# Fourteen pairs of distances between split weights and operands in a dense encoder kernel

## The chip, the cores and the metric

The kernel runs on one core of one Trainium2 chip. The metric is the device time in microseconds of one execution, from the first to the last instruction plus what the launch adds around it; lower is better. A profile of one execution stands beside the times. Engines are named as the profile names them: PE is TensorE (PEld its weight loads), DVE is VectorE, ACT is ScalarE, POOL is GpSimd, SP is SyncE.

## The reference

Two layers over a sequence of 256 positions and 2048 channels, all in float32. Each layer does:

```python
hn = _rmsnorm(h, norm_g[i])
u = hn @ w_in[i]                      # 2048 -> 5632 columns
a_val, a_glu, a_z, q, k, v, b_z = jnp.split(u, offs, axis=-1)
ya = _conformer_conv(a_val, a_glu, conv_w[i], conv_b[i], cln_g[i], cln_b[i])
ya = ya * jax.nn.silu(a_z)
yb = _window_attention(q, k, v, bias_band, sink[i]) * jax.nn.silu(b_z)
h = h + jnp.concatenate([ya, yb], axis=-1) @ w_out[i]
e = _rmsnorm(p[i] @ w_pe[i], pe_g[i])
h = h + e * jax.nn.sigmoid(h @ w_pg[i])
```

`_conformer_conv` is a gated linear unit, a depthwise convolution of width 31, a layer norm and a SiLU; `_window_attention` is banded attention with 16 query heads over 4 key heads. A final RMSNorm closes the trunk. Nearly all of the work is in the four projections `w_in`, `w_out`, `w_pe` and `w_pg`.

## The kernel before

**Layout.** Everything is transposed: channels lie on the 128 partitions, the 256 positions along the free axis. A projection is a sum over 128-channel slices; the weight slice (128x128) is the stationary operand, which TensorE loads, and the activations (128x256) are the moving operand, which it streams.

**Three matmuls for one.** A float32 product is made of three faster fp32r matmuls. Each operand is split into a rounded high part and the low part that is left. `mm3` (L396) issues high x high, high x low and low x high, in that order, into one PSUM accumulation; "high x low" is the high part of the weights with the low part of the activations. So of three weight loads two are of the high part of the weights and one of the low part.

**Half tiles.** The weights come as a list of 156 half tiles for each layer (`HALVES`, made by `weight_halves`), 1024 float32 per partition each, mostly 8 slices of 128 columns. One half tile is 24 matmuls: 8 slices by 3. In the order of the list: 0 to 3 `w_pe`; 4 to 35 value and gate columns of the convolution group (tile ag); 36 to 39 keys (k); 40 to 43 values (v); 44 to 75 attention gate and queries (zb, q); 76 to 91 convolution gate (za); 92 to 107 `w_out` with the attention half (o<-yb); 108 to 123 `w_out` with the convolution half (o<-ya); 124 to 155 `w_pg` (g). In layer 0, half tiles 0 to 3 are used unsplit.

**The weights' way.** `load` (L158) fetches two half tiles in one transfer of 1 MB on the SP queue into one of three raw buffers. `split` (L163) takes one of five buffers of the tile w, has ACT cast the raw values to the high part (L168) and DVE subtract to the low part (L171). `ahead` and `get` (L178 to L195) run the splits up to four half tiles before their use. The order of DVE, PE and ACT instructions is written out by hand; `pump` (L203) is called after each half tile and issues convolution taps (L559) and pieces of the attention between the splits. `step` and `steps` (L406 to L422) walk the cursor over the half tiles and call `mm3`.

**Where things lie.** A buffer of w is 2 x 1024 + 64 float32 (8,448 bytes) per partition and begins at a multiple of 128 bytes. The split starts `SHIFT` = 16 elements, 64 bytes, into it: high part at 64, low part 4,096 bytes further. The activations' split tiles (hg, ya, yb, h1, and pp for `w_pe` in layer 1) begin at multiples of 128 bytes, and each slice of them is 1,024 bytes long. So the address phase modulo 128 of every slice of the activations is 0 and that of every slice of the weights, high or low, is 64. For the values (v) the roles are exchanged: the activations are loaded and the weights streamed. Small tiles lie elsewhere: qq (split queries, loaded) and keys (streamed) at 32, s (loaded for the transposes pt) at 96, ident and ones at 64.

```python
        w = wspl.tile([P, 2 * HALF + 64], F32R, tag="w", name=f"w{h}")
        w = w[:, SHIFT:SHIFT + 2 * HALF].rearrange("p (t n) -> p t n", t=2)
        hi, lo = w[:, 0], w[:, 1]
        nc.scalar.copy(hi, raw)
```

Of the kernel before, what the change touches and what calls it, by code (L numbers as in the profile page):

```python
# [10 lines left out]
F32 = mybir.dt.float32  # L11
# [6 lines left out]
P = 128  # L18
# [10 lines left out]
W_KV = NKV * HD  # L29
# [9 lines left out]
HALF = 1024  # L39
# [9 lines left out]

NB_FIRST = KT  # L50
NSPL = 5
SHIFT = 16
MAN = 'DVE,PE,Activation'
LY = (2, 1)
ORD = 1
# [65 lines left out]
NHALF = len(HALVES)  # L121
# [8 lines left out]
def trunk_kernel(ctx: ExitStack, tc: tile.TileContext, xT, pT, wst, par, gain, relb, sinkp, onehot, out):  # L130
    nc = tc.nc
# [11 lines left out]
    def bigt(name, dt=F32):  # L143

        return big.tile([P, 2, 8, S], dt, tag="big", name=name)

    def halves(t):
        return [t[:, 0], t[:, 1]]

    def bank(name):  # L150
        return ps.tile([P, 2, S], F32, tag="ps", name=name)
# [3 lines left out]
    raws, spl = {}, {}  # L155
# [7 lines left out]
    def split(h):  # L163
        raw = raws[h // 2][:, h % 2, :]
        w = wspl.tile([P, 2 * HALF + 64], F32R, tag="w", name=f"w{h}")
        w = w[:, SHIFT:SHIFT + 2 * HALF].rearrange("p (t n) -> p t n", t=2)
        hi, lo = w[:, 0], w[:, 1]
        nc.scalar.copy(hi, raw)  # L168
        spl[h] = w
        if h not in (4, 5):  # L170
            nc.vector.tensor_sub(lo, raw, hi.bitcast(F32))  # L171

    def first_lo(h):

        w = spl[h]
        nc.vector.tensor_sub(w[:, 1], raws[h // 2][:, h % 2, :], w[:, 0].bitcast(F32))

    def ahead(h):  # L178

        while state["spl"] < min(h, TOT - 1):  # L180
            n = state["spl"] + 1
            while state["raw"] < min(n // 2 + LD - 1, TOT // 2 - 1):
                state["raw"] += 1
                load(state["raw"])
            if HALVES[n % NHALF][0] != "w_pe" or n >= NHALF:
                split(n)
            state["spl"] = n

    def get(h):

        r = h % NHALF
        if r < 12:
            ahead(h + (r | 1) + 2 - r)
        else:
            ahead(h + LS)  # L195
        return spl.pop(h)
# [6 lines left out]
    def pump(taps=None):  # L203
        taps = RATES[(Cursor.h % NHALF > 4 + 32 + 8 + 12) + (Cursor.h % NHALF > 4 + 32 + 8 + 32 + 4)] if taps is None else taps
        state["credit"] += taps
        if ORD:
            sides()
        while state["credit"] >= 1 and conv_q:
            g = conv_q.pop(0)
            try:  # L210
                next(g)
                state["credit"] -= 1
                conv_q.insert(1, g)
            except StopIteration:
                pass
        if not conv_q:
            state["credit"] = 0.0
        if not ORD:
            sides()
# [59 lines left out]
    h = halves(bigt("x"))  # L279
# [95 lines left out]
    def fold(a):  # L375
        t = wk.tile([P, S], F32, name="fold", tag="sg")
        nc.vector.tensor_add(t, a[:, 0, :], a[:, 1, :])
        return t

    def halves_of(a):  # L380
        return [a[:, 0, :], a[:, 1, :]]

    def square_acc(acc, src, first, eng=None):

        if first:
            nc.scalar.activation(acc, src, AF.Square)
            return
        sq = wk.tile([P, 2, S], F32, name="sq", tag="sq", bufs=3)
        nc.scalar.activation(sq, src, AF.Square)
        (eng or nc.gpsimd).tensor_add(acc, acc, sq)  # L390
# [5 lines left out]
    def mm3(o, w, x, start, stop):  # L396


        nc.tensor.matmul(o, w[:, 0], x[:, 0], start=start, stop=False, skip_group_check=True)  # L399
        nc.tensor.matmul(o, w[:, 0], x[:, 1], start=False, stop=False, skip_group_check=True)  # L400
        nc.tensor.matmul(o, w[:, 1], x[:, 0], start=False, stop=stop, skip_group_check=True)  # L401

    class Cursor:
        h = 0

    def step(o, X, start, stop):  # L406

        steps([o], X, [start], stop)

    def steps(os, X, starts, stop):  # L410

        parts = []
        for _ in os:
            name, _, k0, nk = HALVES[Cursor.h % NHALF]
            parts.append(get(Cursor.h).rearrange("p t (k c) -> p t k c", k=nk))
            Cursor.h += 1
        for kk in range(nk):
            k = k0 + kk
            for o, w, start in zip(os, parts, starts):
                mm3(o, w[:, :, kk, :], X[k // 8][:, :, k % 8, :], start and kk == 0, stop and kk == nk - 1)  # L420
        for _ in os:
            pump()  # L422

# [13 lines left out]
    for l in range(DEPTH):  # L437
# [4 lines left out]
        hg = []  # L442
# [16 lines left out]
        def operands(k, n):  # L459
            for k in range(k, k + 2 * n, 2):  # L460
                subs.append(operand(k))
                if len(subs) > 1:
                    subs.pop(0)()

        ecopy = []
        for q in range(4):
            n = Cursor.h
            Cursor.h += 1
            if l:
                w = get(n).rearrange("p t (j k c) -> p t j k c", j=4, k=2)  # L470
            else:
                raw = raws[n // 2][:, n % 2, :].rearrange("p (j k c) -> p j k c", j=4, k=2)
            for jj in range(0, 4, 2):
                j = 4 * q + jj
                b = bank("e")
                for x in range(2):
                    for k in range(2):
                        if l:
                            mm3(b[:, x, :], w[:, :, jj + x, k, :], pp[:, :, k, :], x == 0 and k == 0, k == 1)
                        else:  # L480
                            nc.tensor.matmul(b[:, x, :], raw[:, jj + x, k, :], pf[:, k, :], start=x == 0 and k == 0,
                                             stop=k == 1, skip_group_check=True)
                if l == 0 and j // 2 < 4:
                    for k in (4 * (j // 2), 4 * (j // 2) + 2):
                        if k < KT - 2:
                            square_acc(hacc, h[k // 8][:, k % 8:k % 8 + 2, :], k == 0, nc.vector)
                    if j // 2 == 3:
                        sq = wk.tile([P, 2, S], F32, name="sq", tag="sq", bufs=3)
                        nc.scalar.activation(sq, h[1][:, 6:8, :], AF.Square)
                        hparts = [fold(hacc)] + halves_of(sq)  # L490
                if j // 2 == QQ[l][0]:
                    dg = rstd_col(hparts, D, f"rh{l}")
                    ahead(4 if l == 0 else Cursor.h - 1 - q + 5)
                if j // 2 == QQ[l][1]:
                    rbs.append(rstd_row(dg, f"rh{l}", copy=False))
                    if l == 0:
                        first_lo(4)
                        ahead(5)
                        operands(0, 1)
                        first_lo(5)  # L500
                        subs.pop(0)()
                        operands(2, 1)
                if QQ[l][1] + (l == 0) <= j // 2 <= QQ[l][1] + 1:
                    operands(4 * (j // 2 - QQ[l][1]), 2)
                ecopy.append((j, b))

                while ecopy and (l or j // 2 >= 3):
                    jc, bc = ecopy.pop(0)
                    nc.scalar.copy(e[jc // 8][:, jc % 8:jc % 8 + 2, :], bc)
            pump()  # L510
# [34 lines left out]
        a, zb = halves(az)  # L545
# [42 lines left out]
        b = pair(hg, f"k{l}")  # L588
# [8 lines left out]
        vb = [bank(f"v{l}_{b}") for b in range(2)]  # L597
        for q in range(4):
            n = Cursor.h
            Cursor.h += 1  # L600
            w = get(n).rearrange("p t (k c) -> p t k c", k=4)
            for kk in range(4):
                k = 4 * q + kk
                for b in range(2):
                    mm3(vb[b][:, 0, :], hg[k // 8][:, :, k % 8, b * P:(b + 1) * P], w[:, :, kk, :],
                        k == 0, k == KT - 1)
            pump()
        v = wk.tile([P, 2, W_KV], F32, name=f"v{l}", tag="v", bufs=1)
# [60 lines left out]
        for i in range(0, 8, 2):  # L669

            b = pair(hg, f"zb{l}_{i}")
            nc.scalar.activation(zb[:, i:i + 2, :], b, AF.Silu)
            b = pair(hg, f"q{l}_{i}")
# [3 lines left out]
            for hh in range(2):  # L677
                r, o = rows_of[hh], rows_of[1 - hh]
# [7 lines left out]
        for t in range(0, NCT, 2):  # L686
            b = pair(hg, f"za{l}_{t}")
# [59 lines left out]
        for j in range(0, KT, 2):  # L747
            b = bank(f"o{l}_{j}")
# [6 lines left out]
        for j in range(0, KT, 2):  # L755
# [3 lines left out]
            hi, lo = (x[:, j % 8:j % 8 + 2, :] for x in halves(h1[-1]))  # L759
            b = bank(f"o{l}_{j}")  # L760
# [50 lines left out]
        for j in range(0, KT - 2, 2):  # L811
            if j:
                b = pair(h1, f"g{l}_{j}")
            else:
                b = bank(f"g{l}_{j}")
# [4 lines left out]
            if j == 4 and not last:  # L820
                pp = wk.tile([P, 4 * S + 32], F32R, name="pp", tag="qq")
                pp = pp[:, 24:24 + 4 * S].rearrange("p (x k s) -> p x k s", x=2, k=2)
                hilo(pp[:, 0], pp[:, 1], pf)
        for j in range(KT - 2, KT):
            b = bank(f"g{l}_{j}")[:, 0:1, :]
# [4 lines left out]
        h = e  # L830
# [93 lines left out]
```

## Time and profile before

| | us |
|---|---|
| runs of the kernel | 951.45, 951.17, 944.24 |
| median | 951.17 |
| the profiled execution | 950.28 |
| its span, first to last instruction | 948.5 |
| mean granted TensorE clock in it | 0.997 of full speed |

The page puts the span into busy shares of the engines, a strip of 40 time slices, the DMA queues, the chain of work that ended last, and groups of instructions by line and tile. A group such as `g<-h,w` names the tile written and the tiles read. Bytes moved are 182.55 MB, 192 GB/s over the span. The strip shows TensorE at nine tenths or more in all slices but the first and the last:

```profile
PE   8999999999999999999999999999999999999995
PEld 7999999999999999999999999999999999999995
DVE  3899999998887676776679998999888878677663
ACT  4655455787875554454466444558787555546551
```

Since matmuls are pipelined, "busy" says only that at least one was under way. How many matmuls a stretch holds says how fast TensorE went through it.

### The profile page before, as it was taken

What the parts mean: (1) busy time and instruction counts of PE and PEld (TensorE: products, weight loads), DVE (VectorE), ACT (ScalarE), POOL (GpSimd) and SP (SyncE); (2) the same over time, 40 slices, a digit from 0 to 9 for tenths busy, and PEclk for the clock granted to TensorE, in tenths of its full rate; (3) what the DMA queues carried; (4) which work ended last, traced back from release to release, by engine and by line L of the source; (5) the groups of instructions that cost most, each with busy time, mean ns of one, the idle gap of its engine ahead of it and who ended that gap; (6) DMA issues with size and microseconds to landing.
All of it is one profiled execution on the core that took longest, in us unless ns stands there. A gap on an engine that the chain in (4) does not pass through costs nothing.

```text
span 948.5 us, 19102 instructions
## 1 busy us (share of the span) xinstructions
PE 935.5 (99%) x7952; PEld 918.8 (97%) x7952; DVE 769.4 (81%) x1290; ACT 549.4 (58%) x830; POOL 83.8 (9%) x79
## 2 busy tenths in 40 slices
PE   8999999999999999999999999999999999999995
PEld 7999999999999999999999999999999999999995
DVE  3899999998887676776679998999888878677663
ACT  4655455787875554454466444558787555546551
POOL 0022001010000000011103200000100010000111
PEclk9999999999999999999999999999999999999998
DMA  8674556555456465556555566465454564655532
GB/s 294 226 254 157 200 178 244 195 188 191 168 174 231 171 224 183 178 179 225 189 196 198 174 219 206 154 217 199 167 205 144 190 223 146 246 186 178 191 121 90
DMA packets 29011, 182.55 MB, mean 192 GB/s; under 512 B 3595, under 2 KB 4156, under 8 KB 9084
## 3 DMA queue, kind: packets, MB, share of 16 engines
q1 hardware_dynamic: 24284, 165.70, 49.9%
q0 software_dynamic: 3344, 12.88, 4.2%
q10 hardware_dynamic: 1296, 2.75, 0.8%
q8 instruction: 62, 1.02, 0.4%
q14 instruction: 25, 0.20, 0.1%
HBM read 177.09 MB, written 4.23 MB: 191 GB/s over the span
## 4 chain that ended last, share of the span: by engine, by line
PE 95%; DVE 3%; DMA 1%; issue 0%; ACT 0%; POOL 0%; ACTq 0%; DVEq 0%
PE g L401 6%; PE g L399 6%; PE g L400 6%; PE ag L401 6%; PE ag L399 6%; PE ag L400 6%; PE o L400 6%; PE o L399 6%; PE o L401 6%; PE za L399 3%; PE zb L400 3%; PE za L400 3%; PE zb L401 3%; PE zb L399 3%; PE q L399 3%; PE za L401 3%
## 5 line engine op out<-in xcount | busy, mean ns | idle before, releaser
L171 DVE TENSOR_TENSOR w<-raw,w 128x1024 fp32r<-128x1024 f32 x306 | 373.2, 1228 | 105.1 <-ACT w L168 104.5
L168 ACT CAST w<-raw 128x1024 fp32r<-128x1024 f32 x308 | 316.2, 1046 | 166.3 <-PE ag L401 40.6
L559 DVE SCALAR_TENSOR_TENSOR cz<-az,pars,cz 128x241 f32<-128x241 f32 (+11 forms) x480 | 217.8, 502 | 1.0
L401 PE MATMUL ag<-hg,w 128*128 128x256 f32 x512 | 143.0, 279 | 0.6 <-DVE w L171 0.5
L399 PE MATMUL ag<-hg,w 128*128 128x256 f32 x512 | 142.8, 279 | 0.0
L401 PE MATMUL g<-h,w 128*128 128x256 f32 x512 | 142.6, 279 | 0.0
L399 PE MATMUL g<-h,w 128*128 128x256 f32 x512 | 142.6, 278 | 0.0
L400 PE MATMUL g<-h,w 128*128 128x256 f32 x512 | 142.6, 278 | 0.0
L400 PE MATMUL ag<-hg,w 128*128 128x256 f32 x512 | 142.5, 278 | 0.0
L401 PEld LDWEIGHTS ag<-hg,w 128*128 128x128 f32 x512 | 96.2, 188 | 1.2 <-DVE w L171 1.0
L401 PEld LDWEIGHTS g<-h,w 128*128 128x128 f32 x512 | 97.2, 190 | 0.0
L400 PEld LDWEIGHTS ag<-hg,w 128*128 128x128 f32 x512 | 96.9, 189 | 0.1
L399 PEld LDWEIGHTS ag<-hg,w 128*128 128x128 f32 x512 | 96.1, 188 | 0.9 <-ACT w L168 0.8
L399 PEld LDWEIGHTS g<-h,w 128*128 128x128 f32 x512 | 96.1, 188 | 0.0
L400 PEld LDWEIGHTS g<-h,w 128*128 128x128 f32 x512 | 96.1, 188 | 0.0
L399 PE MATMUL o<-yb,w 128*128 128x256 f32 x256 | 72.2, 282 | 0.0
L399 PE MATMUL za<-hg,w 128*128 128x256 f32 x256 | 72.0, 281 | 0.0
L400 PE MATMUL o<-yb,w 128*128 128x256 f32 x256 | 71.6, 280 | 0.0
L399 PE MATMUL q<-hg,w 128*128 128x256 f32 x256 | 71.5, 279 | 0.0
L401 PE MATMUL o<-yb,w 128*128 128x256 f32 x256 | 71.4, 279 | 0.0
L399 PE MATMUL zb<-hg,w 128*128 128x256 f32 x256 | 71.4, 279 | 0.0
L399 PE MATMUL o<-ya,w 128*128 128x256 f32 x256 | 71.3, 278 | 0.0
(219 smaller groups left out, 2269.4 us busy)
## 6 DMA issues: line engine op xcount, KB each, us to landing
raw<-in_wst SPq DMA_DIRECT2D x153, 1024.0 KB, 4.9
bias<-fscr POOLq DMA_DIRECT2D x16, 384.0 KB, 4.0
raw<-in_wst SPq DMA_DIRECT2D x4, 512.0 KB, 8.0
az<-in_xT POOLq DMA_DIRECT2D x4, 512.0 KB, 5.3
hscr<-e POOLq DMA_DIRECT2D x2, 1024.0 KB, 5.5
az<-hscr POOLq DMA_DIRECT2D x4, 512.0 KB, 5.8
x<-in_xT SPq DMA_DIRECT2D x3, 512.0 KB, 8.2
out_t<-og ACTq DMA_DIRECT2D x4, 256.0 KB, 3.0
```

The source lines that it names most:

```text
L168: nc.scalar.copy(hi, raw)
L171: nc.vector.tensor_sub(lo, raw, hi.bitcast(F32))
L399: nc.tensor.matmul(o, w[:, 0], x[:, 0], start=start, stop=False, skip_group_check=True)
L400: nc.tensor.matmul(o, w[:, 0], x[:, 1], start=False, stop=False, skip_group_check=True)
L401: nc.tensor.matmul(o, w[:, 1], x[:, 0], start=False, stop=stop, skip_group_check=True)
L559: nc.vector.scalar_tensor_tensor(acc[:, t, lo_:hi_], a[:, t, lo_ + s:hi_ + s], w(k), acc[:, t, lo_:hi_], ALU.mult, ALU.add)
```

## The change

The two parts of a split half tile get places of their own. `SHIFT` becomes a pair of byte distances, one for the high and one for the low part, and `shift(h)` picks the pair for half tile h: in each layer seven groups of sixteen consecutive half tiles have a pair from `SHIFTS`, all others have (64, 64). The low part is counted from element `HALF + 32`, so at equal distances it lies 4,224 bytes behind the high one. The size of the buffer is the same. The rest of the diff hands the two parts on as a pair of tiles where one tile with two halves was handed on before; the matmuls and their order are the same.

```diff
-SHIFT = 16
+SHIFT = (64, 64)
+SHIFTS = [
+    [(4, 16, 16), (20, 48, 48), (76, 80, 80), (92, 96, 96), (108, 112, 112), (124, 64, 0), (140, 0, 64)],
+    [(4, 64, 96), (20, 96, 64), (76, 64, 32), (92, 32, 64), (108, 64, 80), (124, 80, 64), (140, 48, 64)],
+]
+
+
+def shift(h):
+
+    for k, a, b in SHIFTS[h // NHALF]:
+        if k <= h % NHALF < k + 16:
+            return a // 4, b // 4
+    return SHIFT[0] // 4, SHIFT[1] // 4
...
     def split(h):
         raw = raws[h // 2][:, h % 2, :]
         w = wspl.tile([P, 2 * HALF + 64], F32R, tag="w", name=f"w{h}")
-        w = w[:, SHIFT:SHIFT + 2 * HALF].rearrange("p (t n) -> p t n", t=2)
-        hi, lo = w[:, 0], w[:, 1]
+        a, b = shift(h)
+        hi, lo = w[:, a:a + HALF], w[:, HALF + 32 + b:2 * HALF + 32 + b]
         nc.scalar.copy(hi, raw)
-        spl[h] = w
+        spl[h] = (hi, lo)
...
     def mm3(o, w, x, start, stop):
 
 
-        nc.tensor.matmul(o, w[:, 0], x[:, 0], start=start, stop=False, skip_group_check=True)
-        nc.tensor.matmul(o, w[:, 0], x[:, 1], start=False, stop=False, skip_group_check=True)
-        nc.tensor.matmul(o, w[:, 1], x[:, 0], start=False, stop=stop, skip_group_check=True)
+        nc.tensor.matmul(o, w[0], x[0], start=start, stop=False, skip_group_check=True)
+        nc.tensor.matmul(o, w[0], x[1], start=False, stop=False, skip_group_check=True)
+        nc.tensor.matmul(o, w[1], x[0], start=False, stop=stop, skip_group_check=True)
```

More of the change, by code (lines that the diff above doesn't have):

```diff
@@ L173, in first_lo @@
     def first_lo(h):
-        w = spl[h]
-        nc.vector.tensor_sub(w[:, 1], raws[h // 2][:, h % 2, :], w[:, 0].bitcast(F32))
+        hi, lo = spl[h]
+        nc.vector.tensor_sub(lo, raws[h // 2][:, h % 2, :], hi.bitcast(F32))
     def ahead(h):
@@ L396, in mm3, with parts_of @@
     def mm3(o, w, x, start, stop):
-        nc.tensor.matmul(o, w[:, 0], x[:, 0], start=start, stop=False, skip_group_check=True)
-        nc.tensor.matmul(o, w[:, 0], x[:, 1], start=False, stop=False, skip_group_check=True)
-        nc.tensor.matmul(o, w[:, 1], x[:, 0], start=False, stop=stop, skip_group_check=True)
+        nc.tensor.matmul(o, w[0], x[0], start=start, stop=False, skip_group_check=True)
+        nc.tensor.matmul(o, w[0], x[1], start=False, stop=False, skip_group_check=True)
+        nc.tensor.matmul(o, w[1], x[0], start=False, stop=stop, skip_group_check=True)
+    def parts_of(x):
+        return [x[:, 0], x[:, 1]]
     class Cursor:
@@ L414, in steps @@
             name, _, k0, nk = HALVES[Cursor.h % NHALF]
-            parts.append(get(Cursor.h).rearrange("p t (k c) -> p t k c", k=nk))
+            parts.append(get(Cursor.h))
             Cursor.h += 1
@@ L419, in steps @@
             for o, w, start in zip(os, parts, starts):
-                mm3(o, w[:, :, kk, :], X[k // 8][:, :, k % 8, :], start and kk == 0, stop and kk == nk - 1)
+                mm3(o, [y[:, kk * P:(kk + 1) * P] for y in w], parts_of(X[k // 8][:, :, k % 8, :]),
+                    start and kk == 0, stop and kk == nk - 1)
         for _ in os:
@@ L469, in trunk_kernel @@
             if l:
-                w = get(n).rearrange("p t (j k c) -> p t j k c", j=4, k=2)
+                w = [y.rearrange("p (j k c) -> p j k c", j=4, k=2) for y in get(n)]
             else:
@@ L478, in trunk_kernel @@
                         if l:
-                            mm3(b[:, x, :], w[:, :, jj + x, k, :], pp[:, :, k, :], x == 0 and k == 0, k == 1)
+                            mm3(b[:, x, :], [y[:, jj + x, k, :] for y in w], parts_of(pp[:, :, k, :]), x == 0 and k == 0, k == 1)
                         else:
@@ L600, in trunk_kernel @@
             Cursor.h += 1
-            w = get(n).rearrange("p t (k c) -> p t k c", k=4)
+            w = get(n)
             for kk in range(4):
@@ L604, in trunk_kernel @@
                 for b in range(2):
-                    mm3(vb[b][:, 0, :], hg[k // 8][:, :, k % 8, b * P:(b + 1) * P], w[:, :, kk, :],
+                    mm3(vb[b][:, 0, :], parts_of(hg[k // 8][:, :, k % 8, b * P:(b + 1) * P]),
+                        [y[:, kk * W_KV:(kk + 1) * W_KV] for y in w],
                         k == 0, k == KT - 1)
```

## The prediction, made before the changed kernel was run

> **What bounds the kernel now.** I read the page first: busy times, the chain that ended last, the costliest groups.
>
> ```profile
> span 948.5 us, 19102 instructions
> ...
> PE 935.5 (99%) x7952; PEld 918.8 (97%) x7952; DVE 769.4 (81%) x1290; ACT 549.4 (58%) x830; POOL 83.8 (9%) x79
> ...
> PE 95%; DVE 3%; DMA 1%; issue 0%; ACT 0%; POOL 0%; ACTq 0%; DVEq 0%
> ...
> L171 DVE TENSOR_TENSOR w<-raw,w 128x1024 fp32r<-128x1024 f32 x306 | 373.2, 1228 | 105.1 <-ACT w L168 104.5
> L168 ACT CAST w<-raw 128x1024 fp32r<-128x1024 f32 x308 | 316.2, 1046 | 166.3 <-PE ag L401 40.6
> ...
> L401 PE MATMUL ag<-hg,w 128*128 128x256 f32 x512 | 143.0, 279 | 0.6 <-DVE w L171 0.5
> ```
>
> TensorE carries 95% of the chain and the waits in front of it are parts of a microsecond. The 279 ns of a matmul is its latency; matmuls overlap, so what counts is the step from one start to the next, which I call the pace. The timeline of a quiet stretch shows it.
>
> ```profile
> 100.00 0.28 PE L400 MATMUL ag<-hg,w 128*128 128x256 f32 x1
> 100.01 0.19 PEld L401 LDWEIGHTS ag<-hg,w 128*128 128x128 f32 x1
> 100.11 1.23 DVE L559 SCALAR_TENSOR_TENSOR cz<-az,pars,cz 128x241 f32<-128x241 f32 x3
> 100.12 0.28 PE L401 MATMUL ag<-hg,w 128*128 128x256 f32 x1
> 100.12 0.19 PEld L399 LDWEIGHTS ag<-hg,w 128*128 128x128 f32 x1
> 100.23 0.28 PE L399 MATMUL ag<-hg,w 128*128 128x256 f32 x1
> ```
>
> Each weight load (PEld) starts 0.01 us or less behind a matmul and belongs to the next one: the load reads w while the matmul reads the operand. So the change can act in one place, the pace, if these two reads disturb each other. To see whether the pace varies, I cut the span at the first matmuls of the fourteen groups that the change moves (window view; 16 half tiles of 24 matmuls = 384 matmuls in each, in the order of the change's two lists; the windows' counts take in a few neighbours).
>
> ```profile
> 23.79:70.65 46.86, 46.23 (x388) 44.68 (x387) 43.43 (x68) 28.28 (x37) 5.89 (x5) 1.00 0.70 240
> 70.65:114.17 43.52, 43.52 (x386) 43.52 (x385) 43.45 (x70) 21.69 (x27) 9.06 (x6) 1.00 0.52 175
> 239.43:293.86 54.43, 54.43 (x464) 51.68 (x463) 44.37 (x93) 38.44 (x72) 2.56 (x4) 1.00 0.54 186
> 293.86:340.66 46.80, 46.71 (x396) 46.48 (x395) 35.71 (x45) 26.27 (x37) 2.68 (x3) 1.00 0.51 182
> 340.66:385.89 45.23, 45.23 (x386) 45.23 (x385) 29.85 (x33) 20.45 (x23) 0.00 (x0) 1.00 0.58 208
> 385.89:431.12 45.23, 45.23 (x387) 45.23 (x385) 34.48 (x45) 22.16 (x25) 2.59 (x2) 1.00 0.53 182
> 431.12:476.34 45.22, 45.22 (x386) 45.22 (x385) 29.69 (x33) 21.45 (x26) 5.79 (x5) 1.00 0.60 215
> 488.54:533.58 45.04, 45.04 (x387) 44.92 (x386) 41.58 (x58) 27.95 (x38) 11.00 (x6) 1.00 0.48 164
> 533.58:578.88 45.30, 45.30 (x393) 45.30 (x392) 45.23 (x81) 19.70 (x24) 4.75 (x3) 1.00 0.61 209
> 704.11:758.70 54.59, 54.59 (x464) 51.84 (x463) 44.45 (x94) 38.45 (x72) 0.56 (x1) 1.00 0.48 166
> 758.70:804.46 45.76, 45.67 (x397) 45.44 (x396) 34.65 (x45) 26.16 (x37) 2.69 (x3) 1.00 0.53 179
> 804.46:847.98 43.52, 43.52 (x387) 43.52 (x386) 30.75 (x34) 20.48 (x23) 0.00 (x0) 1.00 0.62 225
> 847.98:891.50 43.52, 43.52 (x387) 43.52 (x386) 32.74 (x45) 24.08 (x30) 2.59 (x2) 1.00 0.54 187
> 891.50:935.02 43.52, 43.52 (x387) 43.52 (x385) 24.24 (x30) 21.17 (x31) 5.17 (x4) 1.00 0.30 105
> ```
>
> Columns: window and length, busy time and count of PE, PEld, DVE, ACT, POOL, granted clock, DMA share, GB/s. The clock is 1.00 throughout and TensorE is never idle in the pure stretches, yet the same code has two paces. The w_out and w_pg stages of layer 0 (340.66 to 476.34) take 45.23 us for 384 matmuls, 117.8 ns each; the same stages of layer 1 (804.46 to 935.02) take 43.52 us, 113.3 ns, with the same addresses. DVE and DMA do not explain it: in 70.65:114.17 DVE is busy for 43.45 of 43.52 us and the pace is the fast one. So at a distance of 64 bytes TensorE runs in one of two locked paces, 4.5 ns apart. I take the four windows at 43.52 us as 113.3 ns, the four from 293.86 to 476.34 as 117.8 (the first holds a gap besides) and the six others, which hold attention matmuls or gaps and, by their times, both paces, as the middle, 115.5. The mean over the fourteen is (4 x 113.3 + 4 x 117.8 + 6 x 115.5) / 14 = 115.5 ns.
>
> **Is there a price of the address distance?** All groups stand at 64 bytes, so the answer must come from neighbours. In the layout, qq (loaded) and keys (streamed) both start 32 bytes past a multiple of 128: distance 0. The transposes load s at 96 and stream ident at 64: distance 32. The idle matmuls load ones and stream ident, both at 64: distance 0. First two lines of the chain in layer 0 and one in layer 1:
>
> ```profile
> 176.28 0.95 PE sc L627 x8
> ...
> 179.95 0.87 PE pt L654 x8
> ...
> 629.07 0.95 PE sc L627 x8
> ```
>
> And a window over the idle matmuls near the end:
>
> ```profile
> 935.57:936.47 0.90, 0.90 (x10) 0.90 (x9) 0.74 (x2) 0.09 (x1) 0.00 (x0) 1.00 0.00 0
> ```
>
> The scores, at distance 0, take 0.95 / 8 = 119 ns for the same 128x256 shape: 1 above the slow pace and 6 above the fast one. Eight in a row is little, since a lock may need longer. Of the 128-wide ones, transposes at 32 take 0.87 / 8 = 109 ns; the idle matmuls at 0 take 0.90 us for eight steps, 112 ns (its count of 10 includes one at each end). Both pairs say that distance 0 is dearer, by 3 to 6 ns, and the second that 32 is not. The two score rows use the two qq buffers, which lie 4,224 bytes apart, an odd multiple of 128: equal times, so 128 more changes nothing here, and I take the phase modulo 128.
>
> **The change, part by part.**
> - Number of instructions, DMAs, waits, their order: unchanged. The same casts, subtractions and matmuls, on other offsets in the same w tile. No queue is passed by anything.
> - Writes of the split at other offsets (L168, L171): all offsets are multiples of 16 bytes. Nearest rows are the taps of the convolution, whose starts differ by multiples of 4 bytes:
>
> ```profile
> L559 DVE SCALAR_TENSOR_TENSOR cz<-az,pars,cz 128x255 f32<-128x255 f32 x32 | 15.2, 475 | 0.0
> L559 DVE SCALAR_TENSOR_TENSOR cz<-az,pars,cz 128x253 f32<-128x253 f32 x32 | 15.2, 474 | 0.0
> L559 DVE SCALAR_TENSOR_TENSOR cz<-az,pars,cz 128x254 f32<-128x254 f32 x32 | 15.1, 472 | 0.0
> ```
>
> They agree within 3 ns of 475, so I put the split at no change: at most 1% of 1228 ns, about 12 ns per half tile either way, covered by TensorE's 2.7 us per half tile. Where DVE is full (70.65:114.17), that cover is thin: 224 subtractions x 12 ns = 2.7 us would be the most if every one showed. I take 0.
> - The low part's default start moves from 4,096 to 4,224 bytes behind the high one: nothing, by the score rows. Bound: the difference of the two paces, 4.5 ns, on a third of the matmuls outside the groups (7,392 - 5,376 = 2,016): 672 x 4.5 ns = 3 us either way.
> - The distances: 14 x 384 = 5,376 matmuls, so 1 ns of mean pace is 5.4 us. Bounds for each group: 113.3 (fast lock) and 119.4 (distance 0). In mm3 two of three loads read the high part, so it weighs 2/3 and the low part 1/3. For each distance I take the nearest row: 64, 48, 80: both locks occur, 115.5. 32: also 115.5, since the transposes show no price there. 16 and 112, only 16 bytes from 0: 119.4. 96, as far from 0 as from 64 and with no row: the middle, 117.5. 0: 119.4.
>
> Layer 0: (16,16) 119.4; (48,48) 115.5; (80,80) 115.5; (96,96) 117.5; (112,112) 119.4; (64,0) 2/3 x 115.5 + 1/3 x 119.4 = 116.8; (0,64) 118.1. Layer 1: (64,96) 116.2; (96,64) 116.8; (64,32), (32,64), (64,80), (80,64), (48,64) 115.5 each. Sum 1,632.7, mean 116.6, that is 1.1 ns above 115.5, 6 us. Against the profiled execution, 950.28 us (span 948.5 and 1.8 around it, 0.9 below the median 951.17): 950.28 + 6 = 956 us. A slower TensorE gives every other engine more slack; where it became faster than 113.3, DVE would be late next in 70.65:114.17.
>
> **Rivals.**
> 1. The distance does nothing; the paces are a matter of how the two streams happen to lock after a disturbance. For it: both paces at one and the same distance, and three runs of one program from 944.24 to 951.45. Against it: the score and idle rows. Mean pace stays 115.5: 950 us, with the spread of the runs. The Trainium skill says so too (TensorE: Matmul & The Clock Gate, Step-by-step: what each phase is for): matmul operand and weight load have read ports of their own, and loading the next weights takes no bandwidth from the running matmul. By that the change is worth nothing. The trace disagrees in part: 112 against 109 ns in like matmuls. The same page's spacing for isolated matmuls (Back-to-back issue gap: N / 2.4 + 2.5 ns, 109.2 at 256 columns) would make 384 matmuls 41.9 us, an estimate; no window here reaches it.
> 2. Faster: the fourteen switches of distance shake TensorE out of the slow lock, and it stays in the fast one in all groups: 2.2 x 5.376 = 12 us less, 938 us. It decides, by the bound below, once 8.6 of these 12 us come. Against it: the slow lock held for 135 us in layer 0, and the change also touches the stretch that is fast now.
> 3. Clearly slower: every distance other than 64 meets more collisions than 64, and each mixed pair takes the price of its worse half: 119.4 or more everywhere. 3.9 x 5.376 = 21 us, 971 us; above that if a distance is worse than 0. Only the score row speaks for it.
>
> **How the numbers follow.** Forecast 0.45, rival 1 0.32, rival 2 0.07, rival 3 0.16. About 1% (9.5 us) is what a measurement of this kernel can tell from no change: faster means under 941.7, slower over 960.7. The forecast varies by the locks that its groups take, some 5 us either way, so a third of it (0.15) is over 960.7; with rival 3 (0.16) and a little of rival 1 slower is 0.33. Faster is rival 2 with 0.02 of rival 1: 0.09. The rest, 0.58, is within 1%. The range reaches from 943, under the lowest run shown, to 971, rival 3; some 0.08 lies below and 0.10 above. The likeliest case alone: 951 to 961.
>
> **What would show it.** In the changed profile the pace of each group is the time between its first matmul and the next group's, over 384. Right: (16,16), (112,112) and (0,64) near 119 ns and steady, the pairs at 32 to 80 at 113.3 or 117.8. Rival 1: only these two paces, in no relation to the pair. Rival 2: 43.5 us in all pure groups. Rival 3: 45.8 us or more in nearly all. Any wait before a matmul on w that was not there before, or a casting row away from 1046 and 1228 ns, would show that the split's writes were mispriced. A distance at which the pace leaves the bounds of 113.3 to 119.4 would break the sum.

## The result and the profile after

The changed kernel takes 963.5 us (median of 4 runs, 963.13 to 964.47) against 950.95 us before (4 runs, 944.24 to 951.45). The ratio is 1.0154, with a 95% interval of 1.0122 to 1.0186: some 12.6 us slower. The profiled execution took 963.38 us with a span of 961.6 us, 13.1 us longer than the span before.

The page of the changed kernel (busy times, chain, costliest groups) shows a kernel that does the same work in the same order; `split` is now at L180 and L183, `mm3` at L411 to L413.

```profile
span 961.6 us, 19102 instructions
...
PE 949.0 (99%) x7952; PEld 932.1 (97%) x7952; DVE 769.6 (80%) x1290; ACT 549.4 (57%) x830; POOL 82.8 (9%) x79
...
PE 96%; DVE 2%; DMA 1%; ACT 0%; issue 0%; ACTq 0%; DVEq 0%
```

DVE and ACT do the same busy time as before to 0.2 us, TensorE 13.5 us more. The grouped lines show that the writes of the split cost the same.

```profile
L183 DVE TENSOR_TENSOR w<-raw,w 128x1024 fp32r<-128x1024 f32 x306 | 375.2, 1234 | 111.7 <-ACT w L180 111.2
L180 ACT CAST w<-raw 128x1024 fp32r<-128x1024 f32 x308 | 316.3, 1046 | 173.9 <-PE ag L413 45.7 <-PE g L413 29.8 <-PE za L413 23.2
```

The cast takes 1046 ns as before. The subtraction takes 6 ns more, and TensorE waits for it no longer than before (0.2 us in all, 0.5 before). So the time is in the pace of TensorE. The same fourteen windows as before, from one group's first matmul to the next group's (columns as in the prediction):

```profile
25.19:72.36 47.17, 46.98 (x389) 45.76 (x388) 43.54 (x69) 27.91 (x37) 6.58 (x5) 1.00 0.67 238
72.36:118.42 46.06, 46.06 (x386) 46.06 (x385) 45.99 (x74) 21.57 (x27) 8.39 (x6) 1.00 0.53 183
243.59:299.66 56.07, 56.07 (x464) 53.28 (x463) 44.52 (x94) 38.40 (x72) 2.56 (x4) 1.00 0.55 182
299.66:346.48 46.82, 46.82 (x396) 46.61 (x395) 35.73 (x46) 26.27 (x37) 2.68 (x3) 1.00 0.51 181
346.48:391.71 45.23, 45.23 (x387) 45.23 (x385) 29.77 (x33) 20.43 (x23) 0.00 (x0) 1.00 0.58 208
391.71:437.10 45.39, 45.39 (x386) 45.39 (x385) 34.50 (x45) 22.18 (x25) 2.58 (x2) 1.00 0.51 182
437.10:482.33 45.23, 45.23 (x387) 45.23 (x385) 29.71 (x33) 21.47 (x26) 5.79 (x5) 1.00 0.60 214
494.42:539.36 44.94, 44.94 (x387) 44.94 (x386) 41.38 (x58) 27.97 (x38) 11.41 (x6) 1.00 0.47 165
539.36:585.27 45.91, 45.91 (x393) 45.91 (x391) 45.84 (x82) 19.70 (x24) 3.40 (x3) 1.00 0.58 207
709.83:765.63 55.80, 55.80 (x465) 53.00 (x463) 44.53 (x94) 38.40 (x72) 0.56 (x1) 1.00 0.48 164
765.63:812.45 46.82, 46.82 (x397) 46.59 (x396) 35.74 (x46) 26.26 (x37) 2.69 (x3) 1.00 0.51 181
812.45:857.67 45.22, 45.22 (x387) 45.22 (x385) 29.74 (x33) 20.45 (x23) 0.00 (x0) 1.00 0.58 208
857.67:902.90 45.23, 45.23 (x386) 45.23 (x385) 32.84 (x44) 24.05 (x30) 2.58 (x2) 1.00 0.53 183
902.90:948.13 45.23, 45.23 (x386) 45.23 (x385) 24.14 (x30) 21.30 (x31) 5.17 (x4) 1.00 0.27 97
```

None is at 43.52 us any more. The four windows that were fast (second and last three) lost 2.54, 1.70, 1.71 and 1.71 us; those that were slow stayed at 45.23 or close. The six mixed ones grew by 4.7 us together; one of them, the first of layer 1, shrank by 0.1. The fourteen lengths sum to 661.12 us against 648.54, 12.6 us more. That is nearly all of the 13.1: the first matmul on hg comes 1.4 us later (25.19 against 23.79) and the stretches in between, which keep (64, 64), got 0.9 us shorter together. The pace is 44.94 / 384 = 117.0 ns at (64, 96), 45.39 / 384 = 118.2 at (64, 0), 46.06 / 384 = 119.9 at (48, 48) and 117.8 in the other pure windows.

### The profile page after: what moved, and what is told of

Same layout as the page of the kernel before. It is cut to its first block, busy times and chain, and to the rows that moved or that the text cites. A ratio compares the mean times of both kernels' runs of the same rounds, so it can differ in the third digit from the quotient of the medians.

```text
span 961.6 us, 19102 instructions
## 1 busy us (share of the span) xinstructions
PE 949.0 (99%) x7952; PEld 932.1 (97%) x7952; DVE 769.6 (80%) x1290; ACT 549.4 (57%) x830; POOL 82.8 (9%) x79
## 4 chain that ended last, share of the span: by engine, by line
PE 96%; DVE 2%; DMA 1%; ACT 0%; issue 0%; ACTq 0%; DVEq 0%
PE o L411 6%; PE g L412 6%; PE g L411 6%; PE o L413 6%; PE o L412 6%; PE g L413 6%; PE ag L413 6%; PE ag L411 6%; PE ag L412 6%; PE za L412 3%; PE za L411 3%; PE za L413 3%; PE zb L411 3%; PE q L413 3%; PE zb L413 3%; PE q L411 3%
## 5 line engine op out<-in xcount | busy, mean ns | idle before, releaser
L183 DVE TENSOR_TENSOR w<-raw,w 128x1024 fp32r<-128x1024 f32 x306 | 375.2, 1234 | 111.7 <-ACT w L180 111.2
L180 ACT CAST w<-raw 128x1024 fp32r<-128x1024 f32 x308 | 316.3, 1046 | 173.9 <-PE ag L413 45.7
L411 PE MATMUL ag<-hg,w 128*128 128x256 f32 x512 | 144.6, 282 | 0.0
L411 PE MATMUL g<-h,w 128*128 128x256 f32 x512 | 144.2, 282 | 0.0
L413 PE MATMUL ag<-hg,w 128*128 128x256 f32 x512 | 144.0, 281 | 0.2 <-DVE w L183 0.2
L413 PE MATMUL g<-h,w 128*128 128x256 f32 x512 | 143.2, 280 | 0.0
L413 PEld LDWEIGHTS g<-h,w 128*128 128x128 f32 x512 | 97.2, 190 | 0.0
L411 PEld LDWEIGHTS ag<-hg,w 128*128 128x128 f32 x512 | 96.3, 188 | 0.9 <-ACT w L180 0.9
L413 PEld LDWEIGHTS ag<-hg,w 128*128 128x128 f32 x512 | 96.6, 189 | 0.4 <-DVE w L183 0.4
L411 PEld LDWEIGHTS g<-h,w 128*128 128x128 f32 x512 | 96.2, 188 | 0.0
L411 PE MATMUL o<-yb,w 128*128 128x256 f32 x256 | 72.8, 284 | 0.0
L412 PE MATMUL za<-hg,w 128*128 128x256 f32 x256 | 72.7, 284 | 0.0
L411 PE MATMUL za<-hg,w 128*128 128x256 f32 x256 | 72.5, 283 | 0.0
L412 PE MATMUL o<-ya,w 128*128 128x256 f32 x256 | 72.0, 281 | 0.0
L411 PE MATMUL o<-ya,w 128*128 128x256 f32 x256 | 71.9, 281 | 0.0
L412 PE MATMUL o<-yb,w 128*128 128x256 f32 x256 | 71.8, 280 | 0.0
L413 PE MATMUL za<-hg,w 128*128 128x256 f32 x256 | 71.7, 280 | 0.0
```

Source lines behind the costliest of these rows:

```text
L411: nc.tensor.matmul(o, w[0], x[0], start=start, stop=False, skip_group_check=True)
L412: nc.tensor.matmul(o, w[0], x[1], start=False, stop=False, skip_group_check=True)
L413: nc.tensor.matmul(o, w[1], x[0], start=False, stop=stop, skip_group_check=True)
```

## The experiments

The expectations name four theories. A: the pair of distances sets the pace. B: both paces belong to (64, 64), and chance decides which holds. C: the stage sets the pace. D: the price comes from loads that alternate between two distances. A lock is a steady pace that TensorE keeps over many matmuls.

In each run, a group is sixteen half tiles, 384 matmuls; 43.52 us is 113.3 ns each, 45.23 is 117.8 and 46.08 is 120.0. Rows shown are of the window view.

**All half tiles at (64, 64).** The low part stays 4,224 bytes behind the high one; nothing else differs from the changed kernel.

```diff
-SHIFTS = [
-    [(4, 16, 16), (20, 48, 48), ...
+SHIFTS = [[], []]
```

> The changed kernel with (64, 64) for every half tile: the high part at 64 bytes, the low part 4,224 bytes behind it. Theory A (the pace belongs to the pair: (64, 64) in this layout takes 113.3 ns nearly always, every other pair 117 ns or more): the fourteen groups fall from a mean of 118.2 to some 113.5 ns, 5,376 x 4.7 ns = 25 us under the changed kernel, 938 us, and no stage at 117.8. Theory B (both paces belong to (64, 64), whatever the layout, and which one holds is chance): as the kernel before, 944 to 951 us, with long stages at 117.8 ns.

```profile
70.37:113.89 43.52, 43.52 (x386) 43.52 (x385) 43.45 (x70) 21.58 (x27) 9.44 (x6) 1.00 0.50 175
339.00:382.52 43.52, 43.52 (x386) 43.52 (x385) 30.77 (x34) 20.48 (x23) 0.00 (x0) 1.00 0.62 225
382.52:426.04 43.52, 43.52 (x386) 43.52 (x385) 34.39 (x46) 22.20 (x25) 2.60 (x2) 1.00 0.52 185
426.04:469.56 43.52, 43.52 (x386) 43.52 (x385) 29.39 (x33) 21.48 (x26) 5.79 (x5) 1.00 0.62 227
```

940.67 us, median of 10 runs (940.11 to 942.91), against 948.93 before (13 runs, 941.66 to 954.95): ratio 0.9929, 0.9895 to 0.9964. This is as theory A has it. The stages of layer 0 that were slow in the kernel before are fast, and so is every pure group of layer 1. The ten runs lie within 2.8 us, those of the kernel before within 13.3. It is the fastest version by its median; single runs of the kernel before come down to 941.66. Half tiles 44 to 75 keep (64, 64) throughout the experiments on the pairs. In the profiles of the changed kernel, of this run and of the far pairs below they take 102.33 or 102.34 us in both layers, in the kernel before 102.38 and 103.47. The run also parts the change in two. By the medians, moving the low part 128 bytes further is worth about -8 us, and leaving (64, 64) in fourteen groups about +23; for the second the two versions were not run side by side.

**The lists exchanged between the layers.**

```diff
 SHIFTS = [
-    [(4, 16, 16), ...
-    [(4, 64, 96), ...
+    [(4, 64, 96), ...
+    [(4, 16, 16), ...
```

> The two lists of pairs are exchanged between the layers, so that each pair meets the other layer's group of the same number. Theory A (the pair sets the pace): (48, 48) takes 120 ns now in half tiles 20 to 35 of layer 1, (80, 80) 118.8 in 76 to 91 of layer 1, (64, 96) 117.0 in 4 to 19 of layer 0, all others 117.8 as before; total 962 to 965 us. Theory C (the stage sets it): 120 stays in half tiles 20 to 35 of layer 0. Theory B (chance): some of the groups away from (64, 64) come out at 113.3 ns.

```profile
72.92:118.15 45.23, 45.23 (x387) 45.23 (x385) 45.16 (x73) 21.56 (x27) 8.41 (x6) 1.00 0.52 187
493.73:539.20 45.47, 45.47 (x386) 45.47 (x385) 41.71 (x59) 27.97 (x38) 11.10 (x6) 1.00 0.46 163
539.20:585.91 46.71, 46.71 (x393) 46.71 (x391) 45.74 (x82) 19.68 (x24) 3.06 (x3) 1.00 0.57 203
```

963.46 us (2 runs). The dear pair (48, 48) took its price along to layer 1: 46.71 us there (third row; it holds a few other matmuls besides) against 45.91 in the same place before the exchange, and layer 0 has 45.23 where it had 46.06. (16, 16), which shared its window with gaps in the changed kernel, shows 45.47 / 384 = 118.4 ns here. The pair sets the pace, not the stage, and no group away from (64, 64) is fast.

**The kernel before, once more**, without an edit.

> The kernel before, profiled once more. If the lock is chance (theory B), the stages at 117.8 ns lie elsewhere than in the first profile (there 340.66 to 476.34 us was slow and 773 to 935 us fast), and the time is anywhere from 938 to 958 us. If program and addresses decide the lock, the same stages are slow, within a few half tiles, and the time is 950 us.

```profile
340.37:385.60 45.23, 45.23 (x387) 45.23 (x385) 29.77 (x33) 20.46 (x23) 0.00 (x0) 1.00 0.58 208
...
804.06:847.58 43.52, 43.52 (x386) 43.52 (x385) 30.76 (x34) 20.47 (x23) 0.00 (x0) 1.00 0.62 226
```

949.88 us (1 run), and the same stages slow and fast as in the first profile. In these two executions the lock is no coin thrown anew each time: the same program fell into it at nearly the same places. Not everywhere: in layer 1 the slow pace sets in at half tile 8 in the first profile and at half tile 10 in this one. Other executions may differ more; the 13 runs of this kernel taken beside these first experiments went from 941.66 to 954.95.

**Both parts at 192 bytes, low part 4,096 behind.** In the kernel before:

```diff
-SHIFT = 16
+SHIFT = 48
```

> The kernel before with SHIFT = 48: both parts at 192 bytes, the low part 4,096 behind the high one, phase 64 modulo 128 as before. If the phase counts modulo 128, both paces as before, 944 to 951 us. If it counts modulo 256, 192 is another distance and, by theory A, takes 117 ns or more: 7,392 x 118 instead of 115.5 is 18 us more, 968 us.

```profile
345.60:389.12 43.52, 43.52 (x387) 43.52 (x385) 30.80 (x34) 20.46 (x23) 0.00 (x0) 1.00 0.62 224
...
899.19:944.41 45.22, 45.22 (x386) 45.22 (x385) 24.13 (x30) 21.29 (x31) 5.17 (x4) 1.00 0.28 97
```

960.83 us (4 runs; ratio to the kernel before 1.0126, 1.0070 to 1.0182), between the two expectations. Both paces occur, at places other than before: layer 0's late stages are fast, layer 1's slow. So 192 can lock both ways as 64 can, and here the slow one held longer.

**Fine steps around (64, 64).** Fourteen pairs, edit of `SHIFTS` alone, e.g.

```diff
+    [(4, 60, 60), (20, 68, 68), (76, 56, 56), (92, 72, 72), (108, 64, 60), (124, 64, 68), (140, 60, 64)],
+    [(4, 68, 64), (20, 64, 72), (76, 64, 56), (92, 72, 64), (108, 56, 64), (124, 128, 64), (140, 192, 64)],
```

> Fourteen pairs close to (64, 64), in steps of 4 and 8 bytes, in the same groups as the change: layer 0 (60, 60), (68, 68), (56, 56), (72, 72), (64, 60), (64, 68), (60, 64); layer 1 (68, 64), (64, 72), (64, 56), (72, 64), (56, 64), (128, 64), (192, 64). Theory A narrow (only the exact pair has the fast pace): all fourteen at 117 ns or more, total 962 to 967 us. Theory A wide (a window of some bytes around 64): the pairs at 4, perhaps at 8 bytes, take 113.3 ns, total 945 to 952 us. The pair (128, 64) is at 117 or more under both; (192, 64) puts both parts at 192 bytes modulo 256, as the run with SHIFT = 48 did, and can take either pace.

```profile
71.77:117.01 45.24, 45.24 (x387) 45.24 (x385) 45.17 (x73) 21.58 (x27) 8.43 (x6) 1.00 0.51 186
345.62:391.12 45.50, 45.50 (x387) 45.50 (x386) 29.34 (x32) 20.43 (x23) 0.00 (x0) 1.00 0.56 204
391.12:437.17 46.05, 46.05 (x387) 46.05 (x385) 34.59 (x45) 22.18 (x25) 2.59 (x2) 1.00 0.49 181
437.17:483.25 46.08, 46.08 (x387) 46.08 (x385) 29.86 (x33) 21.46 (x26) 5.77 (x5) 1.00 0.57 209
```

965.41 us (1 run). The rows are (68, 68), (64, 60), (64, 68) and (60, 64): 117.8, 118.5, 119.9 and 120.0 ns. Four bytes off in one part alone cost as much as anything in the change. No pure window of the fourteen groups comes down to 43.52 us, which is the narrow reading of theory A. The pair (192, 64), which could have taken either pace, ran at 117.8.

**The parts exchanged, low part first.** All half tiles at (64, 64), so modulo 256 the high part lies at 192 and the low part at 64.

```diff
-        hi, lo = w[:, a:a + HALF], w[:, HALF + 32 + b:2 * HALF + 32 + b]
+        lo, hi = w[:, a:a + HALF], w[:, HALF + 32 + b:2 * HALF + 32 + b]
```

> All half tiles at (64, 64) with the two parts exchanged: the low part lies first, at 64 bytes, the high part 4,224 behind it, so modulo 256 the high part is at 192 and the low part at 64. If it is the difference of 128 bytes between the parts that leaves only the fast lock, 113.3 ns in all stages, 938 to 943 us. If the fast lock wants the high part at 64 modulo 256, both paces or the slow one, 945 to 966 us.

```profile
343.81:389.47 45.66, 45.66 (x387) 45.66 (x385) 29.59 (x32) 20.42 (x23) 0.00 (x0) 1.00 0.57 205
...
812.97:856.49 43.52, 43.52 (x387) 43.52 (x386) 30.75 (x33) 20.48 (x23) 0.00 (x0) 1.00 0.60 224
```

959.63 us (2 runs; ratio 1.0117, 1.0036 to 1.0198): both paces again, the slow one at 45.66 / 384 = 118.9. A difference of 128 bytes between the parts isn't enough; it matters which of them lies at 64. The edit also exchanges which part comes first in the buffer, and no run parts the two.

**Kicks in the kernel before.** One idle 128x128 matmul ahead of every second pair of tiles in the w_pg stage; these come to three in each layer, not the four that the expectation names. The profile shows each as two matmuls, 12 more than the 18 of the kernel before.

```diff
         for j in range(0, KT - 2, 2):
+            if j % 4 == 2:
+                idle(1)
             if j:
```

> The kernel before with one idle 128x128 matmul ahead of every second pair of tiles in the w_pg stage, four in each layer, 0.1 to 0.2 us each. If the pace is a lock that holds until TensorE's stream is disturbed (theory B), the pace in half tiles 124 to 155 changes at some of the eight places, 117.8 to 113.3 in layer 0 or the reverse in layer 1. If data or addresses of the stage set it, layer 0 stays at 117.8 and layer 1 at 113.3, and the time rises by 1 us.

```profile
386.13:397.44 11.31, 11.31 (x99) 11.31 (x98) 8.36 (x12) 6.00 (x6) 0.00 (x0) 1.00 0.53 187
397.57:419.44 21.87, 21.87 (x196) 21.87 (x195) 16.66 (x22) 10.44 (x12) 1.29 (x1) 1.00 0.55 189
430.56:474.32 43.76, 43.76 (x389) 43.76 (x388) 29.37 (x33) 21.48 (x26) 5.79 (x5) 1.00 0.61 223
```

948.91 us (1 run). The first row is four half tiles up to the first kick: 11.31 / 96 = 117.8 ns. The second is the eight half tiles behind it up to the next kick: 21.87 / 192 = 113.9, which holds the restart of some 0.1 us; without it 113.3. One idle matmul at 397.44 set TensorE free, and it stayed fast to the end of the layer (third row, one more kick in it). The w_pg stage of layer 1 was fast ahead of its kicks and remained so. The slow pace at 64 bytes is a lock that persists until the stream is disturbed, and not a property of the stage. This is one kick, but the profile of the kernel before bears it out. Followed step by step, it changes between the two paces some thirty times. Each time a matmul of another kind or a step of 0.2 us or more stands in between, but for two changes, at 137.04 and 600.64, where the values end, for which the weights are the streamed operand.

**(48, 48) throughout.**

```diff
-SHIFT = (64, 64)
+SHIFT = (48, 48)
-SHIFTS = [
+SHIFTS = [[], []]
```

> (48, 48) for every half tile. Theory A (each pair has its pace wherever it stands, and the paces add up): 120 ns in all stages, 7,392 x (120.0 - 113.4) = 49 us above the kernel with (64, 64) throughout, 989 us. Theory C (the stage sets the pace): 120 only in half tiles 20 to 35, some 965 us.

```profile
353.79:399.87 46.08, 46.08 (x386) 46.08 (x385) 29.35 (x32) 20.43 (x23) 0.00 (x0) 1.00 0.55 202
...
504.57:549.80 45.23, 45.23 (x386) 45.23 (x385) 41.44 (x57) 27.96 (x38) 10.96 (x6) 1.00 0.47 164
```

982.34 us (2 runs), 42 us over all-(64, 64) where 49 were expected. The pace is 120.0 in most stages, which excludes theory C, but one group of layer 1 runs at 117.8: this pair too has two paces, both above the fast one.

**Kicks in the changed kernel**, the same edit as above.

> The changed kernel with the same eight idle matmuls in the w_pg stages (half tiles 124 to 155: pairs (64, 0), (0, 64) in layer 0, (80, 64), (48, 64) in layer 1). If these pairs have no fast lock at all (theory A), the pace stays at 117.8 to 118.2 ns behind every kick and the time rises by some 1 us, 964.5. If the slow pace there is only the lock that TensorE happened to fall into (theory B), some of the eight kicks set it free and stretches at 113.3 ns appear, each half tile of them 0.1 us shorter.

```profile
392.69:404.03 11.34, 11.34 (x98) 11.34 (x97) 8.36 (x12) 6.00 (x6) 0.00 (x0) 1.00 0.54 186
404.17:426.96 22.79, 22.79 (x196) 22.79 (x194) 16.80 (x22) 10.43 (x12) 1.28 (x1) 1.00 0.53 185
```

965.75 us (1 run). Four half tiles ahead of a kick take 11.34 / 96 = 118.1 ns, eight behind it 22.79 / 192 = 118.7 with the restart. The same kick that freed (64, 64) frees nothing at (64, 0), nor do the others at (0, 64), (80, 64) and (48, 64).

**The high part alone.** The kernel leaves out the low part's product and loads the high part a third time. `SHIFTS` puts the high part of the fourteen groups at 0, 16, ... 208 bytes, in order, and the low part, which is written but not read, at 128.

```diff
-SHIFT = (64, 64)
+SHIFT = (64, 128)
...
-        nc.tensor.matmul(o, w[1], x[0], start=False, stop=stop, skip_group_check=True)
+        nc.tensor.matmul(o, w[0], x[0], start=False, stop=stop, skip_group_check=True)
```

> The third matmul of mm3 takes the high part of the weights again in place of the low part, so the low part's product is left out and every load has one distance; the fourteen groups stand at 0, 16, ... 96 bytes (layer 0) and 112, 128, ... 208 (layer 1), all other half tiles at 64. If each distance has its own price (theory A), the groups at 64 and, by the run at 192, at 192 show 113.3 ns, those at 0, 48 and 128 some 120, the others 117 to 119, and the time is 958 to 965 us. If the price comes from loads that alternate between two distances (theory D), a single distance locks at 113.3 ns wherever it is, and the time is 938 to 943 us.

```profile
345.71:390.94 45.23, 45.23 (x386) 45.23 (x385) 29.70 (x32) 20.44 (x23) 0.00 (x0) 1.00 0.57 208
...
494.18:540.25 46.07, 46.07 (x386) 46.07 (x385) 42.11 (x60) 27.96 (x38) 12.62 (x6) 1.00 0.49 166
...
905.37:950.17 44.80, 44.80 (x387) 44.80 (x386) 24.11 (x30) 21.28 (x31) 5.19 (x4) 1.00 0.28 98
```

965.43 us (1 run). The rows are 64, 112 and 208 bytes: 117.8, 120.0 and 116.7 ns. Theory D falls: one distance for all loads is no cure. Theory A was wrong in its figures too: the group at 64 sat in the slow lock, and 48 came to 118.1 here, over the steps of its group without a gap, against 120.0 in the pair (48, 48). The price of a pair isn't read off from its parts.

**Fourteen pairs far from (64, 64)**, edit of `SHIFTS` alone.

> Fourteen pairs far from (64, 64), counted as the change counts them (the low part from 4,224 bytes on): layer 0 (0, 0), (0, 128), (128, 0), (128, 128), (32, 32), (160, 64), (176, 64); layer 1 (192, 128), (192, 80), (208, 80), (208, 128), (208, 96), (224, 112), (224, 128). Theory A (of all pairs only those with both parts at 64 modulo 128 can run at 113.3 ns): all fourteen between 116.6 and 120 ns, 960 to 968 us. If the fast pace needs only some difference between the two parts, or if there is a still better place, some group shows 113.3 ns or less, 1.8 us or more off the time for each.

```profile
73.64:119.71 46.07, 46.07 (x386) 46.07 (x385) 46.00 (x74) 21.55 (x27) 9.45 (x6) 1.00 0.52 183
...
904.33:949.27 44.94, 44.94 (x386) 44.94 (x385) 24.12 (x30) 21.31 (x31) 5.16 (x4) 1.00 0.28 97
```

964.52 us (1 run). No group is at 113.3 ns; the pure windows lie between 44.94 us, (224, 128), and 46.07 us, (0, 128), that is 117.0 and 120.0 ns. So among the pairs tried, theory A's reading stands.

## Why the prediction was right or wrong

**Where the change can act: right.** Only TensorE's pace moved. The writes of the split cost nothing that shows, no wait came in, the other engines kept their busy times.

**The distances: right in sign, half the size, wrong in order.** The forecast was a mean pace 1.1 ns higher, 6 us; the fourteen windows grew by 12.6 us, 12.6 / 5.376 = 2.3 ns. The step that failed is "64, 48, 80: both locks occur, 115.5", and 32 beside it. Seven of the fourteen pairs were priced as if each could fall into the fast lock like (64, 64); none stayed in it. (48, 48) came to 119.9, (64, 80), (80, 64) and (48, 64) to 117.8, 2.3 ns over the forecast. The transposes, by which 32 was put at no price, hold 128-column matmuls, and their 109 ns did not carry over to 256 columns: the windows of (64, 32) and (32, 64) grew by 1.2 and 1.1 us. Near distance 0 the error had the other sign: 119.4 was taken for (16, 16) and (112, 112), 118.4 and 117.8 were measured. The 119.4 itself is above its row, 0.95 / 8 = 118.8.

So the order of the distances was wrong. The pairs near 0 were to be the dear ones, those at 32 to 80 were to have the two paces at 64. In fact (112, 112) and (0, 64) ran at 117.8 like (64, 80) and (80, 64), and (48, 48), one of the cheap ones by the forecast, was dearest at 119.9, outside the bounds of 113.3 to 119.4. The forecast drew its rise from the price of distance 0; the measured rise came from all fourteen pairs alike. That its sign was right is in part luck, and 963.5 us lies in the range because the range reaches up to rival 3.

**The phase modulo 128: wrong.** The step "128 more changes nothing here", read from two equal score rows, was the basis for putting the low part's new default at nothing, 3 us either way. In the stages outside the groups it was indeed worth only 0.9 us, but (64, 64) with 4,096 between the parts has two locks, and with 4,224 it stayed in the fast one in every group. Over the whole kernel that is worth some 8 us. The score rows had only eight matmuls at a pace near 119 ns and could not show a lock.

**Rival 1 (the distance does nothing)** falls by the exchange of the lists and by (48, 48) throughout. Its half-truth, that the two paces at 64 are a lock, is shown by the kick. The Trainium skill (TensorE: Matmul & The Clock Gate, Step-by-step: what each phase is for) spoke for it: by that section, loading the next weights takes no bandwidth from the running matmul. The trace does not agree as far as time goes, since the weights' addresses alone moved the same program from 940.67 to 982.34 us; which read waits, it does not show. **Rival 2** (a switch shakes the slow lock loose) fails for the changed pairs. **Rival 3** (every other distance is dearer than 64) was right for all fourteen pairs, with too high a price: 117 to 120 ns, not 119.4 or more everywhere. Its clause that a mixed pair takes the price of its worse half fails: (48, 64) and (64, 64) make 117.8 and 113.3, (48, 48) makes 119.9.

What stays open is why. That loads and streamed reads disturb each other is the natural reading, since nothing but the weights' addresses changed. But the activations stayed at phase 0 in every run, so it is not shown that the distance between the two counts, and not the weights' own place. Nor does a run tell which of the two reads waits, or why 64 and 192 modulo 256, in this order, leave only the fast lock. Whether a pair exists that runs below 113.3 ns was tried only at the places named.

## What to carry to other kernels

In a stretch where TensorE never waits, divide the length by the number of matmuls, stage by stage: two paces in the same code at the same clock are a sign of a lock, which the busy share of 99% hides. When a layout offset has been found good, treat it as a point and not as a region: here 4 bytes off, in one of the two parts of the weights, cost 4 to 7 ns per matmul. Compare layouts over whole stages and several runs, and price a layout by rows of the same shape and a long stream.

## What the runs showed of the hardware that was not expected

Three paces, 113.3, 117.8 and 120.0 ns, recur to 0.1 ns in pairs that have nothing else in common; the others found lie between 116.7 and 118.9.

More work can take less time: in the kernel before, half tiles 124 to 155 of layer 0 took 90.45 us (385.89 to 476.34), and with the three kicks among them 88.19 (386.13 to 474.32).

The start of the program differs from execution to execution, whatever the distances. In the changed kernel's profile TensorE's granted clock over 14 to 24 us was 0.83, in the kernel before 1.00 (first row):

```profile
14.00:24.00 10.00, 8.46 (x47) 7.26 (x46) 7.39 (x13) 6.93 (x12) 0.70 (x1) 1.00 0.81 272
...
14.00:24.00 10.00, 8.25 (x38) 6.78 (x37) 6.46 (x11) 6.80 (x11) 0.70 (x1) 0.83 0.69 256
```

With it the first matmul on hg came 1.4 us later. The thirteen profiles fall into two kinds: six have 0.83 in that stretch and this matmul at 25.2 to 25.5 us, seven have 1.00 and 23.5 to 23.9. Both kinds occur in the kernel before (at 192 bytes 25.53 us) and in the changed one (with the fine steps 23.82), and up to that point TensorE has read no split weights. So this is no effect of the change.
